# A decoder block on one core: the state-space scan in an order written out by hand, and two memory units in full precision

## The chip, the core and the metric

The kernel runs on one core of a Trainium2 chip. The core has a matrix engine (TensorE, PE in the profile), a vector engine (VectorE, DVE), a scalar engine (ScalarE, ACT) and a general engine (GpSimd, POOL). SyncE (SP) issues most transfers between the main memory and the on-chip memory, SBUF; TensorE writes its results to PSUM. The metric is the device time in microseconds (us). The kernel before takes 1956.74 us as the median of 3 runs (1956.26 to 1957.37).

## The reference

One block of a decoder over 1024 tokens of width 1024, in float32:

```python
def hybrid_mixer(n, w_in, ...):
    z, xBC, dt_raw, q, k, v, r, a1, g_ssd, g_gla = jnp.split(n @ w_in, idx, axis=-1)
    y_ssd = ssd_mixer(z, xBC, dt_raw, ...)
    y_gla = gla_mixer(q, k, v, r, a1, ...)
    merged = sigmoid(g_ssd) * (y_ssd @ w_up_ssd) + sigmoid(g_gla) * (y_gla @ w_up_gla)
    return merged @ w_o

h = h + hybrid_mixer(rmsnorm(h, norm_mix), ...)
h = h + mem_cross_attention(rmsnorm(h, norm_xattn), rmsnorm(mem, norm_mem), ...)
h = h + swiglu(rmsnorm(h, norm_ffn), w_ffn_in, w_ffn_out)
return rmsnorm(h, norm_final)
```

ssd_mixer is a state-space scan: a causal convolution of four taps and a silu over x, B and C; then, chunk by chunk, the masked product of C and B with decay factors exp(cs_t − cs_s) applied to x, plus C times the state carried from the chunks before; a skip term, a gate by silu(z), and an rmsnorm over each of two groups of 512 channels. gla_mixer is a linear attention with a gate per channel, whose logarithm is summed up within chunks. mem_cross_attention attends to 256 fixed memory tokens, whose keys and values come from mem @ w_xkv.

## The kernel before, in words

**Products.** Nearly all matrix products are full-precision products in three passes of a faster number format, fp32r: each operand is split into a high part (a copy by ScalarE, `whi`, line 221) and the rest (a subtraction by DVE, `wlo`), and high×high, high×low and low×high are accumulated. A `Unit` computes 256 output channels for all 1024 tokens by a scheme of seven products instead of eight (B11, B21, T1, B22, T2, T3, T4), each of 12 matmuls of 128x512 into an accumulator `acc`; DVE adds most accumulators into the output (`o<-acc,o`). The weights' sums for the products (`sa`) are made by DVE or POOL.

**Stages.** In the order of the program: the head (memory, x's transposes, keys and values of the memory, and the projection v); the z units, with the preparation of both scans beside them; six xBC units with the convolution; the SSD scan, with units of r, q, k and the first gate unit beside it; the GLA scan, with more gate units; and then the up projections, w_o, cross-attention and feed-forward part.

**The head.** `kv_unit` (line 548) computes 256 of the 2048 key and value columns of the memory. There are eight such units, n = 0 to 7, the values first. `mh` and `ml` are the high and low parts of the memory; a unit splits its weights `raw` in four steps (one `whi` and one `wlo` of 128x512 each) and makes 48 matmuls of 256 columns. Its result goes through `kvs` to the main memory (`vm_d` or `kT_d`). Units 0 and 1 run alone, the next ones beside x's preparation `x_steps`: transposes of x, copies by ScalarE (`xs`), the normed blocks `hs` by DVE, and stores of the copies to `xT_d` by SP. `v_steps` then runs the same seven products for v, with kv units beside it in the banks.

**The scan.** An item is one chunk of 128 tokens of one of the two groups; there are 16. `load` fetches x and z (`xz`), B and C (`bc`) and the running sums of the decay for all partitions (`csb`). `lay` makes C·B and the transposes on TensorE, masks the former into `cbm` and scales x by dt into `xd`. `decay` makes the decay factors `e` (eight ScalarE operations, an exponential), multiplies them by cbm and csb by C. `scan` issues 16 matmuls per kind for the output and two for the state, and updates the state. `gate`, `stat` and `norm` finish the item: skip term and gate (`y`), squares and sums (`sq`, `rd`), a matmul against ones (`stat`), the power by POOL (`rs`), a spreading transpose and the scaling.

**What sets the order.** `run(main, (side, rate))` advances the side generator by `rate` steps for each product of the main units; the tile scheduler then simulates the program and orders the instructions of each engine by priority and readiness, so that the written order is only a starting point. `ahead()` raises the priority of the instructions in it; `pinned` keeps the written order for one instruction. In the scan, 16 items of four steps stand beside nine units of seven products. Tiles with a tag and a number of buffers (`bufs`) are reused in turn: a writer waits for the last reader of the buffer's former content, a transfer among them.

Of the kernel before, what the change touches and what calls it, by code (L numbers as in the profile page):

```python
# [78 lines left out]
def block_kernel(ctx: ExitStack, tc: tile.TileContext, t: dict, out: bass.AP):  # L79
# [467 lines left out]

    def kv_unit(c0):
# [24 lines left out]
        s = stg.tile([P, 2, 256], F32, name="kvs", tag="st")  # L573
# [10 lines left out]
    def x_steps():  # L584
# [4 lines left out]
        for j in range(2):  # L589
# [8 lines left out]
            for k in range(NB):  # L598
# [9 lines left out]
                if k % 4 == 3:  # L608
                    SP.dma_start(xT_d[(k - 3) * P:(k + 1) * P, half(j)].rearrange("(k p) s -> p k s", p=P), xs)
# [26 lines left out]
    def v_steps():  # L636
        for pr in range(2):
# [13 lines left out]
            for n, name in enumerate(CHAIN):  # L651
                parts = []
                with ahead():
# [5 lines left out]
                    elif name == "T3":  # L659
# [123 lines left out]
    def gla_prep():  # L783
# [34 lines left out]
        for h in range(4):  # L818
# [23 lines left out]
    xu = [Unit(w_in, 0, XBC0 + 256 * u) for u in range(6)]  # L842
# [6 lines left out]
    run(singles(zu, B, xu[:1]), (prep, 33 / 28))  # L849
# [4 lines left out]
    cvp = pool("conv", 1, stack=st2)  # L854
    pend = iter(())
    for u in range(6):
        run(group([xu[u]], B, (xu + ru)[u + 1:u + 2]), (pend, 1.0))
        drain(pend)
        pend = conv(u, xu[u])
    drain(pend)  # L860
    st2.close()


    st3 = ExitStack()
    sp_ = pool("ssd", 1, stack=st3)
    state = [sp_.tile([P, GH, 64], F32, name=f"state{g}", tag=f"state{g}") for g in range(2)]
# [5 lines left out]
    class SSD:  # L872
# [8 lines left out]
        def load(s):  # L881
            g, tk = s.g, s.tk
            s.L = sp_.tile([P, 8, CH], F32, name="xz", tag="xz", bufs=3)
            SP.dma_start(s.L[:, 0:4], xbc_d[g * 512:(g + 1) * 512, tk].rearrange("(k p) s -> p k s", p=P))
            s.BC = sp_.tile([P, 2, CH], F32, name="bc", tag="bc", bufs=2)
            for i in range(2):
                r0 = 1024 + i * 256 + g * P
                SP.dma_start(s.BC[:, i], xbc_d[r0:r0 + P, tk])
            s.csb = sp_.tile([P, GH, CH], F32, name="csb", tag="csb", bufs=2)
            SP.dma_start(s.csb.rearrange("p h s -> p (h s)"),  # L890
                         cs_d[s.i0:s.i0 + GH, :].rearrange("h s -> (h s)").partition_broadcast(P))
            SP.dma_start(s.L[:, 4:8], sz_d[g * 512:(g + 1) * 512, tk].rearrange("(k p) s -> p k s", p=P))

        def lay(s):
            p = bank()
# [12 lines left out]
        def decay(s):  # L908
# [8 lines left out]
            mul(DVE, s.e, s.e, s.cbm.unsqueeze(1).to_broadcast([P, GH, CH]))  # L917

        def scan(s):
# [13 lines left out]
            add(DVE, st, p.rearrange("p (h d) -> p h d", d=64), st)  # L933

        def gate(s):
# [5 lines left out]
            sq = sp_.tile([P, 4, CH], F32, name="sq", tag="sq", bufs=1)  # L941
            ACT.activation(sq, s.y, AF.Square)
            s.rd = sp_.tile([P, CH], F32, name="rd", tag="rd", bufs=2)
            add(DVE, sq[:, 0:2], sq[:, 0:2], sq[:, 2:4])
# [14 lines left out]
    def ssd_steps():  # L959
        it = [SSD(c, g) for c in range(NCH) for g in range(2)]  # L960
        it[0].load()
        yield
# [3 lines left out]
        yield  # L966
        for i in range(len(it) + 1):
            z = it[i - 1] if i else None
            a = it[i] if i < len(it) else None
            b = it[i + 1] if i + 1 < len(it) else None  # L970
            if b:
                b.load()
            if a:
                a.scan()
            yield
            if z:
                z.stat()
            if b:
                b.lay()
            yield  # L980
            if a:
                a.gate()
            yield
            if z:
                z.norm()
            if b:
                b.decay()
# [713 lines left out]
```

## Time and profile before

| | |
|---|---|
| median of 3 runs | 1956.74 us |
| profiled execution | 1956.3 us |
| its span on the core | 1954.5 us |
| granted TensorE clock, mean | 0.996 |
| TensorE busy | 1919.9 us (98%) |
| DVE busy | 1317.2 us (67%) |
| ScalarE busy | 848.4 us (43%) |
| POOL busy | 574.1 us (29%) |

The sums in the prediction are made against the profiled execution. A row of a group reads: line, engine, operation, output<-inputs by name, shape, how often, then busy time and mean ns of one, then the engine's idle time just before them and what ended most of it. Nearly every instruction is recorded in a helper, so most rows have line 51 (matmuls), 55 (transposes), 73 (DVE and POOL) or 221 (the high part of a split), and the names tell them apart. The stages in this profile: head with v 0 to 166 us, z units to about 240, xBC units to about 388, SSD scan to about 630, GLA scan to 788, the rest to 1954.

### The profile page before, as it was taken

The page shows a single profiled execution, that of the slowest core. Times are in us where ns is not written, and L with a number is a line of the kernel's source. Part 1 is how long each engine was busy: PE and PEld are TensorE (multiplying, and loading weights), DVE is VectorE, ACT ScalarE, POOL GpSimd, SP SyncE. Part 2 cuts the span into 40 slices and gives each one's busy share as a digit, 9 for nine tenths or more (in the row PEclk, how much of TensorE's full clock was granted, in tenths as well). Part 3 has the DMA queues.
Part 4 walks back from the last instruction along what each step waited for, and adds up shares of the span by engine and source line. Part 5 has one row for each costly group of instructions (what it writes and reads, how often), then busy time and mean ns, then how long its engine had stood idle before and what let it go on. Part 6 is the DMA issues. An engine that isn't in the chain of part 4 may idle for free.

```text
span 1954.5 us, 26271 instructions
## 1 busy us (share of the span) xinstructions
PE 1919.9 (98%) x9772; PEld 1617.3 (83%) x9772; DVE 1317.2 (67%) x1868; ACT 848.4 (43%) x1493; POOL 574.1 (29%) x429
## 2 busy tenths in 40 slices
PE   8899999999999999999999999999999999999998
PEld 7898788778788888888888888888888888888887
DVE  6866779879886655565545237577777777766565
ACT  8434564465552543643224226454333333344243
POOL 1012334355553212112433000006445544320002
PEclk9999999999999999999999999999999999999999
DMA  9333372366553653897684201442233224177463
GB/s 316 139 121 101 119 290 98 133 196 198 169 168 114 209 162 119 328 371 252 242 298 150 78 24 44 140 141 81 87 125 112 82 100 143 42 270 243 159 222 119
DMA packets 238242, 317.97 MB, mean 163 GB/s; under 512 B 16906, under 2 KB 156404, under 8 KB 238116
## 3 DMA queue, kind: packets, MB, share of 16 engines
q1 hardware_dynamic: 238116, 316.31, 47.8%
q8 instruction: 77, 1.26, 0.3%
q14 instruction: 49, 0.40, 0.1%
HBM read 215.27 MB, written 100.99 MB: 162 GB/s over the span
## 4 chain that ended last, share of the span: by engine, by line
PE 83%; DVE 8%; DMA 3%; issue 2%; ACT 2%; POOL 2%; SPq 1%; POOLq 0%; DVEq 0%; ACTq 0%
PE acc L51 72%; PE bank L51 9%; DVE wlo L73 2%; DVE cv L73 1%; PE bank L55 1%; DVE o L73 1%; DMA xt<-in_x_dram 1%; DMA csb<-cs_d 1%; DVE hs L73 1%; DMA raw<-in_w_in_dram 1%; POOL sa L73 0%; ACT e L911 0%; POOL y L73 0%; POOL ssum L73 0%; DVE y L73 0%
## 5 line engine op out<-in xcount | busy, mean ns | idle before, releaser
L51 PE MATMUL acc<-hl,wd 128*128 128x512 f32 x1920 | 438.7, 390 | 0.0
L51 PEld LDWEIGHTS acc<-hl,wd 128*128 128x128 f32 x1920 | 360.4, 188 | 74.1
L73 DVE TENSOR_TENSOR wlo<-raw,whi 128x512 fp32r<-128x512 f32 x272 | 241.6, 894 | 80.7 <-ACT whi L221 78.7
L221 ACT ACTIVATE whi<-raw 128x512 fp32r<-128x512 f32 x272 | 169.5, 628 | 245.1 <-PE acc L51 214.3
L73 DVE TENSOR_TENSOR o<-acc,o 128x512 f32<-128x512 f32 (+1 forms) x256 | 172.8, 676 | 119.8 <-PE acc L51 108.2
L51 PE MATMUL acc<-fs 128*128 128x512 f32 (+1 forms) x792 | 155.7, 356 | 0.1
L51 PEld LDWEIGHTS acc<-fs 128*128 128x128 f32 x792 | 130.8, 189 | 20.7 <-issue 0.5
L73 POOL TENSOR_TENSOR raw<-raw,sa 128x512 f32<-128x512 f32 x44 | 58.7, 1334 | 228.6 <-DVE wlo L73 228.6
L73 DVE TENSOR_TENSOR fs<-fr,fs 128x1024 fp32r<-128x1024 f32 (+1 forms) x84 | 99.0, 1219 | 36.6 <-ACT fs L221 36.5
L221 ACT ACTIVATE fs<-fr 128x1024 fp32r<-128x1024 f32 (+1 forms) x84 | 78.8, 982 | 96.3 <-PE acc L51 32.1
L221 ACT ACTIVATE whi<-sa 128x512 fp32r<-128x512 f32 x96 | 60.0, 626 | 108.3 <-PE acc L51 102.7
L73 POOL TENSOR_TENSOR sa<-raw 128x512 f32<-128x512 f32 x43 | 67.8, 1577 | 105.0 <-DMA raw<-in_w_in_dram 78.0
L73 DVE TENSOR_TENSOR wlo<-sa,whi 128x512 fp32r<-128x512 f32 x96 | 82.2, 857 | 15.2 <-ACT whi L221 15.1
L73 DVE TENSOR_TENSOR wd<-raw,wd 128x1024 fp32r<-128x1024 f32 x40 | 53.1, 1329 | 50.9 <-ACT wd L221 50.8
L73 POOL TENSOR_TENSOR rstd<-rstd,mhalf 128x4 f32<-128x4 f32 (+1 forms) x7 | 8.7, 1246 | 251.2 <-DVE rstd L73 251.2
L221 ACT ACTIVATE wd<-raw 128x1024 fp32r<-128x1024 f32 x40 | 42.3, 1059 | 88.5 <-PE acc L51 82.7
L51 PE MATMUL acc<-B22h,wlo 128*128 128x512 f32 x192 | 76.6, 399 | 3.0 <-DVE wlo L73 3.0
L51 PE MATMUL acc<-T3h,wlo 128*128 128x512 f32 x192 | 76.0, 396 | 1.2 <-DVE wlo L73 1.2
L73 POOL TENSOR_TENSOR raw<-raw 128x512 f32<-128x512 f32 x44 | 75.9, 1725 | 2.8 <-DVE sa L73 2.8
L51 PE MATMUL acc<-T4h,whi 128*128 128x512 f32 x192 | 76.1, 396 | 0.4 <-DVE o L73 0.4
L51 PE MATMUL acc<-B22h,whi 128*128 128x512 f32 x192 | 76.1, 396 | 0.0
L51 PE MATMUL acc<-B11h,whi 128*128 128x512 f32 x192 | 75.8, 395 | 0.0
(389 smaller groups left out, 4735.4 us busy)
## 6 DMA issues: line engine op xcount, KB each, us to landing
raw<-in_w_in_dram SPq DMA_DIRECT2D x26, 1024.0 KB, 5.7
raw<-in_w_ffn_in_dram SPq DMA_DIRECT2D x22, 1024.0 KB, 8.1
act_d<-o SPq DMA_DIRECT2D x77, 256.0 KB, 2.2
fr<-act_d SPq DMA_DIRECT2D x35, 512.0 KB, 5.8
pre<-in_w_ffn_out_dram SPq DMA_DIRECT2D x11, 1024.0 KB
fr<-down_d SPq DMA_DIRECT2D x20, 512.0 KB, 4.7
down_d<-pre SPq DMA_DIRECT2D x33, 256.0 KB, 3.6
raw<-in_w_xkv_dram SPq DMA_DIRECT2D x8, 1024.0 KB, 8.1
```

Of the source, the lines that this page charges most:

```text
L51: return s.e.matmul(o, x, y, **kw)
L55: return s.e.transpose(o, x, i)
L73: return f(*a, **kw)
L221: ACT.activation(hi, src, AF.Copy)
```

## The change

- Head: POOL adds mh and ml into `mf`. kv units 2 and 3 multiply the unsplit weights by mf in full precision: 16 matmuls of 256 columns each, no split. kvs has one buffer instead of three. ScalarE issues the four stores of x's copies instead of SP. v's third difference stands at product T2 instead of T3.
- GLA's preparation makes one scan instruction of 1024 columns for a head instead of two of 512, with one step fewer; the rate beside the z units is 1.0 instead of 33/28.
- The xBC units come in the order 4, 5, 0 to 3 (B and C first), and the first item's data are loaded during the last of them.
- The SSD scan has other steps (some 80 for 70 products), B and C come in one transfer, csb comes a step later, cbm stays in the PSUM bank of C·B, gate and scan are split (gate, square, sum; scan, update). TensorE's instructions keep the written order in this stage. One gate unit moves here from the GLA stage: ten units and five instead of nine and six.

```diff
+    mf = stg.tile([P, NB, MEM], F32, name="mf", tag="mf", bufs=1)
+    for k in range(0, NB, 2):
+        add(POOL, mf[:, k:k + 2], mh[:, k:k + 2], ml[:, k:k + 2])
...
+        whole = n in (2, 3)
         for kk in range(4):
+            if whole:
+                for i in range(2):
+                    o = pa[i][:, :256]
+                    for k in (2 * kk, 2 * kk + 1):
+                        x, y = (raw[:, k], mf[:, k]) if c0 < D else (mf[:, k], raw[:, k])
+                        PE.matmul(o, x[:, i * P:(i + 1) * P], y, start=k == 0, stop=k == 7)
+                yield
+                continue
...
-        s = stg.tile([P, 2, 256], F32, name="kvs", tag="st")
+        s = stg.tile([P, 2, 256], F32, name="kvs", tag="st", bufs=1)
...
-                    SP.dma_start(xT_d[(k - 3) * P:(k + 1) * P, half(j)].rearrange("(k p) s -> p k s", p=P), xs)
+                    ACT.dma_start(xT_d[(k - 3) * P:(k + 1) * P, half(j)].rearrange("(k p) s -> p k s", p=P), xs)
...
-                    elif name == "T3":
+                    elif name == "T2":
                         sub(DVE, A21, A11, A21)
...
-            for j in range(2):
-                pinned(DVE.tensor_tensor_scan(y[:, half(j)], keep[:, half(j)], x[:, half(j)], 0.0, ALU.mult, ALU.add))
-                yield
+            pinned(DVE.tensor_tensor_scan(y, keep, x, 0.0, ALU.mult, ALU.add))
+            yield
...
-    run(singles(zu, B, xu[:1]), (prep, 33 / 28))
+    run(singles(zu, B, xu[:1]), (prep, 1.0))
...
-            s.cbm = sp_.tile([P, CH], F32, name="cbm", tag="cbm", bufs=2)
-            mul(DVE, s.cbm, p[:, :P], triu)
...
-            mul(DVE, s.e, s.e, s.cbm.unsqueeze(1).to_broadcast([P, GH, CH]))
+            cbm = s.p[:, 2 * P:3 * P]
+            mul(DVE, cbm, s.p[:, :P], triu)
+            mul(DVE, s.e, s.e, cbm.unsqueeze(1).to_broadcast([P, GH, CH]))
...
+        for i in range(n + 2):
+            y, z, a, b, c = (it[k] if 0 <= k < n else None for k in range(i - 2, i + 3))
             if a:
                 a.scan()
+            if z:
+                z.sum()
+            if y:
+                y.norm()
+            yield
+            if c:
+                c.load()
+            if b:
+                b.lay()
+            if a:
+                a.gate()
             yield
             if z:
                 z.stat()
             if b:
+                b.decay()
+            if c:
+                c.load_cs()
             if a:
+                a.update()
+            for _ in range(3 if i == 0 else 1):
+                yield
+            if a:
+                a.square()
+                yield
...
-    run(singles(ru + qk + gs[:1], B, gs[1:2]), (ssd, 16 * 4 / 63), prio=PRIO)
+    with tc.manual_schedule(engines={mybir.EngineType.PE}):
+        run(singles(ru + qk + gs[:2], B, gs[2:3]), (ssd, 79 / 70), prio=PRIO)
...
-    run(singles(gs[1:] + gg[:3], B, gg[3:]), (gla, 8 * 5 / 36), prio=PRIO)
+    run(singles(gs[2:] + gg[:3], B, gg[3:]), (gla, 8 * 5 / 30), prio=PRIO)
```

How the instructions move on the engines. First TensorE in the scan, around an item's state matmuls (`xc,bt`), before; `rd` belongs to the norm of the item ahead, `bc` to the next item, `xz` are the transposes of its x:

```order
L51 MATMUL bank<-e,xd 64x128 x2
L51 MATMUL bank<-csb,state_3538 64x128 x2
L51 MATMUL bank<-xc,bt 128x256
L51 MATMUL bank<-ones,rd 128x1
L51 MATMUL bank<-bc 128x128
L55 MATMUL bank<-ident,bc 128x128
L51 MATMUL bank<-xc,bt 128x256
L51 MATMUL acc<-B11h,wlo 128x512
```

After the change, the same place:

```order
L51 MATMUL bank<-e,xd 64x128 x2
L51 MATMUL bank<-csb,state_2552 64x128 x2
L51 MATMUL bank<-xc,bt 128x256 x2
L51 MATMUL bank<-ident,rs 128x128
L51 MATMUL acc<-B11h,whi 128x512
L51 MATMUL acc<-B11l,whi 128x512
L51 MATMUL acc<-B11h,wlo 128x512
```

Before, the scan's matmuls have those of other steps between them, and a product is cut into pieces by the blocks; after, the state's matmuls and the spreading of rs stand together, and then come the 12 matmuls of a whole product, before `bc` and the four transposes of xz; 12 more follow before `ones,rd`, and 12 or 24 before the next scan.

DVE in the scan, before, for one item:

```order
L73 TENSOR_SCALAR rs<-bank 128x1
L73 TENSOR_TENSOR cbm<-bank,triu 128x128
L73 TENSOR_TENSOR e<-e,cbm 128x1024
L73 TENSOR_TENSOR state_3539<-bank,state_3539 128x512
L73 TENSOR_TENSOR o<-acc,o 128x512
L73 TENSOR_TENSOR sq<-sq 128x256
L73 TENSOR_TENSOR rd<-sq 128x128
L73 TENSOR_TENSOR xd<-bank,dtv 128x512
L73 TENSOR_TENSOR o<-acc,o 128x512
```

After:

```order
L73 TENSOR_TENSOR xd<-bank,dtv 128x512
L73 TENSOR_TENSOR wlo<-raw,whi 128x512
L73 TENSOR_TENSOR bank<-bank,triu 128x128
L73 TENSOR_TENSOR o<-acc,o 128x512
L73 TENSOR_TENSOR e<-e,bank 128x1024
L73 TENSOR_SCALAR rs<-bank 128x1
L73 TENSOR_TENSOR state_2551<-bank,state_2551 128x512
L73 TENSOR_TENSOR csb<-csb,bc 128x1024
```

The masked product is now in a bank, and from xd to csb stand eight instructions in one row, of which the next scan needs the last; the sums sq and rd stand outside of it.

In the head, DVE between two groups of splits, before (`hs` are x's normed blocks, `B21l` the low part of a split of them):

```order
L73 TENSOR_TENSOR wlo<-raw,whi 128x512
L73 TENSOR_TENSOR B21l<-hs,B21h 128x512 x2
L73 COPY cols<-bank 128x90
L73 TENSOR_TENSOR hs<-hs 128x512
L73 TENSOR_TENSOR B21l<-hs,B21h 128x512 x2
L73 TENSOR_TENSOR hs<-hs 128x512
L73 SCALAR_TENSOR_TENSOR hs<-xs,cols,rbc 128x512
L73 TENSOR_TENSOR hs<-hs 128x512
L73 SCALAR_TENSOR_TENSOR hs<-xs,cols,rbc 128x512 x2
L73 TENSOR_TENSOR wlo<-raw,whi 128x512
```

After:

```order
L73 TENSOR_TENSOR B21l<-hs,B21h 128x512 x2
L73 TENSOR_TENSOR hs<-hs 128x512
L73 COPY cols<-bank 128x90
L73 SCALAR_TENSOR_TENSOR hs<-xs,cols,rbc 128x512 x3
L73 TENSOR_TENSOR T1l<-hs,T1h 128x512 x4
L73 TENSOR_TENSOR hs<-hs 128x512 x11
L73 TENSOR_TENSOR wlo<-vraw,whi 128x528
L73 TENSOR_TENSOR wlo<-raw,whi 128x512
```

The splits of a kv unit that stood among x's blocks are gone, and the first split of weights comes after the four blocks T1l and eleven differences of hs.

More of the change, by code (lines that the diff above doesn't have):

```diff
@@ L853, in block_kernel @@
     st2 = ExitStack()
[L854 to L861, printed above, removed]
     st3 = ExitStack()
-    sp_ = pool("ssd", 1, stack=st3)
-    state = [sp_.tile([P, GH, 64], F32, name=f"state{g}", tag=f"state{g}") for g in range(2)]
+    sl_ = pool("ssdl", 1, stack=st3)
+    state = [sl_.tile([P, GH, 64], F32, name=f"state{g}", tag=f"state{g}") for g in range(2)]
     for g in range(2):
@@ L959, in ssd_steps @@
     def ssd_steps():
-        it = [SSD(c, g) for c in range(NCH) for g in range(2)]
-        it[0].load()
-        yield
+        n = len(it)
+        it[1].load()
+        it[1].load_cs()
+        for _ in range(1):
+            yield
         it[0].lay()
```

66 lines of the change are left out of this document (38 added, 28 removed).

## The prediction

> **What bounds the kernel now.** I read the page first (shares, chain), then busy time by stage, then each stage's waits. The shares of the span, and the chain that ended last, by engine:
>
> ```profile
> span 1954.5 us, 26271 instructions
> PE 1919.9 (98%) x9772; PEld 1617.3 (83%) x9772; DVE 1317.2 (67%) x1868; ACT 848.4 (43%) x1493; POOL 574.1 (29%) x429
> PE 83%; DVE 8%; DMA 3%; issue 2%; ACT 2%; POOL 2%; SPq 1%; POOLq 0%; DVEq 0%; ACTq 0%
> ```
>
> TensorE is the bound, with 34.6 us idle in all (1954.5 − 1919.9). Busy is not peak, so the stages come next. Windows; columns: stretch and length, then PE, weight load, DVE, ACT, POOL busy us (instructions), granted clock, DMA share, GB/s:
>
> ```profile
> 0.00:40.00 40.00, 31.45 (x237) 28.75 (x237) 20.62 (x37) 33.09 (x65) 3.86 (x12) 1.00 0.91 301
> 40.00:60.00 20.00, 14.13 (x95) 13.56 (x96) 20.00 (x33) 13.81 (x29) 2.84 (x2) 0.84 1.06 376
> 160.00:240.00 80.00, 76.90 (x350) 61.44 (x349) 54.54 (x77) 41.86 (x67) 26.74 (x32) 0.98 0.36 121
> 388.00:600.00 212.00, 208.15 (x1325) 169.73 (x1324) 176.34 (x284) 118.77 (x259) 114.91 (x89) 1.00 0.58 181
> 600.00:788.00 188.00, 188.00 (x942) 159.59 (x941) 110.39 (x220) 81.13 (x195) 48.55 (x40) 1.00 0.47 149
> ```
>
> The change touches 0–60 (head), 160–240 (z units), 388–600 (SSD scan); what follows 788 it leaves alone. The columns alone of the scan do not show what is lost. Same view for the products (tile acc), in the scan and in a stretch of the feed-forward part that never waits; then the chain of waits through one item of the scan:
>
> ```profile
> 388.00:600.00 212.00, 153.34 (x615) 112.99 (x614) 24.47 (x36) 8.64 (x15) 1.00 0.58 181
> 1400.00:1612.00 212.00, 212.00 (x937) 175.70 (x936) 38.35 (x56) 12.75 (x22) 1.00 0.29 97
> 569.64 2.97 PE bank L51 x38
> 572.61 0.11 PE bank L55
> 572.72 0.43 PE bank L51 x2
> 573.15 4.10 PE acc L51 x18
> 577.25 0.44 PE bank L55 x4
> 577.69 0.94 PE acc L51 x4
> 578.62 0.22 PE bank L51 x2
> ```
>
> A product matmul at full rate takes 212/937 = 0.2263 us, so 615 of them need 139.1. An item's own matmuls take 2.97+0.11+0.43+0.44+0.22 = 4.17 us. The tile below has 16 items, the first at 397.3 and the last at 587.7, 12.7 us apart; about 15 fall in the window: 62.6 us. What TensorE loses there is 212 − 139.1 − 62.6 = 10.3 us.
>
> **The scan.** DVE is busy 176 of these 212 us, some 11.8 of each 12.7 us item less the gaps, so it sets which short waits TensorE sees. Groups of DVE (busy, mean ns | idle before), then one tile by min/median/max, then TensorE's waits (sum, count, longest):
>
> ```profile
> L73 DVE TENSOR_TENSOR wlo<-raw,whi 128x512 fp32r<-128x512 f32 x44 | 39.8, 907 | 12.9 <-ACT whi L221 12.9
> L73 DVE TENSOR_TENSOR o<-acc,o 128x512 f32<-128x512 f32 x43 | 29.3, 681 | 12.0 <-PE acc L51 12.0
> L73 DVE TENSOR_TENSOR csb<-csb,bc 128x1024 f32<-128x1024 f32 x16 | 20.0, 1248 | 4.8 <-ACT csb L913 4.7
> L73 DVE TENSOR_TENSOR xd<-bank,dtv 128x512 f32<-128x512 f32 x16 | 10.9, 681 | 0.0
> L73 DVE TENSOR_TENSOR state<-bank,state 128x512 f32<-128x512 f32 x16 | 10.9, 681 | 4.3 <-POOL state L73 4.3
> L73 DVE TENSOR_TENSOR cbm<-bank,triu 128x128 f32<-128x128 f32 x16 | 4.5, 279 | 1.8 <-PE bank L55 1.8
> L73 DVE TENSOR_SCALAR rs<-bank 128x1 f32<-128x1 f32 x16 | 2.4, 148 | 0.2 <-PE bank L51 0.2
> L73 DVE TENSOR_TENSOR e<-e,cbm x16: 1225/2126/2155, 397.3 to 587.7; 128x1024 f32<-128x1024 f32 x16
> PE bank L51 <- POOL rs L73: 2.2, 3, 0.9
> ```
>
> (a) cbm stays in PSUM. The same multiply takes 1.2 us at its quickest and 2.1 at its median; o<-acc,o, with one operand in PSUM, is even. I take 1.25 for e (bounds 1.23 and 2.13): with a mean near 1.94, 0.7 us an item less, 11 us of DVE over 16 items. The page "SBUF — State Buffer" of the Trainium skill, section "Who interferes with whom", says that a DVE instruction with two SBUF inputs contends with a GpSimd instruction that reads SBUF, and one with a single SBUF input does not; the spread of this row agrees, though no run here separates it. By that rule the move to PSUM is worth just this; csb<-csb,bc keeps two SBUF inputs and could inherit the wait.
>
> (b) More room. With ten units (70 products) under 16 items instead of nine, an item has, in the order, 36 or 48 products' matmuls beside it in turn, 42 on average against some 37 before: 42×0.2263+4.17 = 13.7 us for DVE's 11.1. The tenth unit comes from the next stage, where TensorE is busy 188 of 188 us and DVE 110, so nothing is lost or won there.
>
> (c) TensorE's order is fixed as written. Blocks of an item now stand between whole products of 12. In a short item 24 products' matmuls (5.43 us) and the stat matmul lie between the transposes of x and the next scan. In that time DVE does, by its order: xd 0.68, wlo 0.91, the mask multiply 0.28, o 0.68, e 1.25, rs 0.15, the state's update 0.68, csb 1.25: 5.9 us. The scan is then some 0.5 us late in each of the 8 short items (4 us), with about 1 us at the edges: 5 us lost instead of 10.3, **a gain of 5.3**. Bounds: nothing lost, gain 10.3; e at its median of 2.1, 1.4 us late, 8×1.4 = 11.2 lost, 0.9 slower. I take 5 since o, xd and the state's update, each with one operand in PSUM, keep one length beside the same work of POOL, as e now should. Behind a late scan all of TensorE's products stand, and behind those DVE's o; the lateness does not grow, since the long item that follows has 2.7 us (12 matmuls) more than it needs.
>
> (d) The rest: one load fewer an item on SP's queue, item 0's loads moved into the conv stage, the split of gate and scan. The loads land ahead of use now (no DMA among the scan's waits on DVE above), so nothing.
>
> **The head.** TensorE, ScalarE (ACT) and DVE in order of time (start, length, what it waited for), a price of full precision from the GLA stage, and groups of POOL and of stores:
>
> ```profile
> 49.30 0.28 PE L51 MATMUL bank<-whi,mh 128*128 128x256 f32 x1
> 54.85 0.58 PE L51 MATMUL bank<-wlo,mh 128*128 128x256 f32 x1 [5.27 <-DVE wlo L73]
> 55.23 0.42 PE L51 MATMUL bank<-whi,ml 128*128 128x256 f32 x1
> 39.62 2.11 ACT L605 ACTIVATE xs<-bank 128x512 f32<-128x512 f32 x4
> 47.15 0.68 DVE L73 TENSOR_TENSOR wlo<-raw,whi 128x512 fp32r<-128x512 f32 x1
> 54.11 0.68 DVE L73 TENSOR_TENSOR wlo<-raw,whi 128x512 fp32r<-128x512 f32 x1
> 650.90 0.60 PE L51 MATMUL bank<-v,attm 128*128 128x256 f32 x2
> 651.34 0.59 PE L51 MATMUL bank<-sm,qk 128*128 128x256 f32 x2
> L73 POOL TENSOR_TENSOR sa<-sa,raw 128x512 f32<-128x512 f32 x8 | 13.8, 1723 | 0.3
> L582 SPq DMA_DIRECT2D vm_d<-kvs x4: 359/370/3319, 36.5 to 62.8; - x4
> act_d<-o SPq DMA_DIRECT2D x77, 256.0 KB, 2.2
> down_d<-pre SPq DMA_DIRECT2D x33, 256.0 KB, 3.6
> ```
>
> DVE is busy all of 40–60. Between two splits, 47.15 to 54.11, it makes the x blocks, and TensorE waits 5.27 us for the second one. After the hole the matmuls take 0.42–0.58 instead of 0.28, and the window's clock is 0.84. The page "TensorE: Matmul & The Clock Gate", section "What's actually happening", of the Trainium skill says that an idle TensorE drops to half its clock after a few us: the rows agree. By it a hole of 3 to 4 us left behind would cost the slow matmuls too.
>
> Units 2 and 3 in full precision: such a matmul of 256 columns (two records) takes 0.44 us, from the starts 650.90 and 651.34, so a unit takes 16×0.44 = 7.0 us of TensorE against 48×0.113 = 5.4 (half of a 512-wide product). Unit 2's 1.6 us lie in the 8.6 us that TensorE idles before 40; unit 3's in the hole. DVE loses unit 3's four splits, 4×0.68 = 2.7 us, out of the stretch that it fills; unit 2's four went before that. So DVE is some 3 us ahead at the next split that TensorE needs (unit 4's), and **the head ends 3 us sooner**. Upper bound: the hole and its slow clock, 5.27 + 0.75, 6 us; below: nothing, or 1.5 us lost if a hole of the same kind opens in front of unit 4.
>
> Its costs. Four adds for mh+ml on POOL at 1.72 us, 6.9 us, while POOL works 3.9 of the first 40; unit 2 comes behind two units of 5.4 us each and takes the sum two blocks at a time. The kvs buffer is now a single one: ScalarE's copies of unit 1 wait for unit 0's store, issued at 36.5, and those of unit 2 for unit 1's. A store of 256 KB lands 2.2 to 3.6 us after its issue elsewhere, longer perhaps at the DMA share of 1.06 here. By ScalarE's order unit 1's copies now stand behind B11's and beside this run of x's copies (39.62), so the wait is up to 1 us; unit 1's store is then out by 42 to 45, unit 2's copies free its two accumulators at 46 to 49. Until then TensorE has, by its order, 24 matmuls of v, unit 3's 7 us and 12 more of v: from 42 on, some 11 us. Hidden, with 4 us to spare; if that cover goes, v waits for its accumulators and the 3 us go with it. x's four stores leave SP's queue for ScalarE's: 0.4 us each by the issue row, 1.5 us on an engine that works 13.8 of the 20 us; SP's own next loads no longer stand behind them. v's third difference stands earlier in the text, and stood there already in DVE's order: nothing.
>
> **The z units.**
>
> ```profile
> PE acc L51 <- DVE wlo L73: 3.1, 2, 1.9
> L73 DVE TENSOR_TENSOR_SCAN gy<-keep,gx x8: 1199/1216/2244, 213.1 to 248.8; 128x512 f32<-128x512 f32 x8
> ```
>
> One scan of 1024 for two of 512: about 2.4 us either way, but now wlo cannot slip between the halves. The side work also comes later (rate 1.0 for 1.18). Bounds: all of 3.1 gained, or two more waits of 1.2, 2.4 lost; nearest the middle, **0.4 gained**.
>
> **The sum** is against the profiled execution, 1956.3 us (its median of runs is 1956.74, 0.44 above): 1956.3 − 5.3 − 3 − 0.4 = 1947.6; as a median 1948.0.
>
> **The rivals.** A difference of 0.2%, 3.9 us, is about what a measurement of this kernel can tell from none.
> - *More goes.* TensorE's lost 10.3 us vanish as the longer items give DVE 2.6 us of slack each, and the head's hole goes whole: 1956.3 − 10.3 − 6 − 0.4 + 0.4 = 1940. For it: DVE's load falls to 11.1/13.7 = 81%. Against: in the short items the 5.9 us do not fit 5.4.
> - *The holes only move.* e keeps its 2.1 us, or csb takes the contention over: 11.2 lost instead of 10.3; the head saves nothing, since v waits for the kvs stores: about 1957. For it: the median of e is near its maximum, POOL is busy over half of the scan. Against: o<-acc,o's evenness.
> - *The other side: the fixed order stalls TensorE.* Before, products' matmuls stood between the parts of an item's blocks; now a block whose operand is late holds everything behind it. If each of 16 items is 1.6 us late (POOL's rs, up to 0.9 in the row above, with the 0.7 of e), 25.6 are lost for 10.3: 1956.7 + 15.3 − 3.4 = 1969. It decides above (10.3+3.4)/16 = 0.86 us an item, and is slower by 0.2% from 1.1. For it: rs goes through DVE and POOL between two TensorE blocks. Against: between stat and norm now stand 12 or 24 products' matmuls and a scan, 5.7 us or more.
>
> **How the numbers follow.** The forecast 0.50; more goes 0.20; the holes only move 0.13; the stall 0.17. Faster 0.70, same 0.13, slower 0.17. The range takes in the first three: 1937 (1940 less the z units' 3) to 1958 (the moved holes with up to 2 us of the z units' loss).
>
> **What would show it.** In the profile after: e at about 1.25 us, even; TensorE's products in the scan at 42 an item with under 6 us lost by the same sum; the stage one unit longer, the next one shorter; in the head no wait of 5 us on wlo near 50 and a clock above 0.84 in that window; no ScalarE wait over 2 us on the kvs store. I am wrong if TensorE waits for DVE's csb or e by a microsecond in most items, if e stays at 2.1, or if the hole reappears whole at unit 4.

## The result, and the profile after

The changed kernel takes 1962.9 us as the median of 8 runs (1958.75 to 1968.08), the one before 1957.05 us over 8 runs; the ratio is 1.0029, with a 95% interval of 1.0020 to 1.0038. The change makes the kernel 0.3% slower. The forecast was 1948.0 us, in a range of 1937 to 1958.

The profiled execution of the changed kernel is its quickest run, 1958.75 us with a span of 1957.0; the times of the eight runs go with the granted clock, with a mean of 0.996 to 0.998 in the four below 1962 us and of 0.994 or 0.995 in the four above 1964. The page, after: the span, and the busy time of the engines.

```profile
span 1957.0 us, 26169 instructions
PE 1919.1 (98%) x9740; PEld 1617.7 (83%) x9740; DVE 1303.7 (67%) x1856; ACT 845.3 (43%) x1485; POOL 568.7 (29%) x433
```

TensorE idles 37.9 us in all (1957.0 − 1919.1) where it idled 34.6. Windows of the changed kernel, with the columns of the prediction:

```profile
0.00:60.00 60.00, 48.63 (x305) 44.81 (x306) 39.15 (x67) 42.10 (x82) 9.66 (x18) 0.97 0.94 326
160.00:240.00 80.00, 78.35 (x360) 62.65 (x359) 56.24 (x74) 42.31 (x67) 28.32 (x34) 1.00 0.37 124
388.00:620.00 232.00, 223.08 (x1420) 184.37 (x1420) 177.02 (x300) 117.87 (x256) 118.13 (x94) 1.00 0.51 162
800.00:900.00 100.00, 97.57 (x430) 80.23 (x429) 56.34 (x68) 50.62 (x74) 13.06 (x8) 1.00 0.95 347
```

The scan and the stretch behind GLA in the kernel before:

```profile
388.00:620.00 232.00, 228.15 (x1433) 185.87 (x1432) 188.15 (x305) 123.72 (x267) 119.14 (x93) 1.00 0.56 174
800.00:900.00 100.00, 100.00 (x443) 82.86 (x442) 64.99 (x72) 48.67 (x70) 18.38 (x12) 1.00 0.93 343
```

The head and the z units idle less than before (11.4 us for 14.4, the difference of 60.00 and the busy time, and 1.7 for 3.1). The scan idles 8.9 us where it idled 3.9, with 11 us less of DVE's work in it. And after the GLA scan there is a hole that was not there at all. First DVE's multiplies by e and by csb in the scan, after, with its splits of weights (`wlo`), and TensorE's waits there; then TensorE's waits from 640 to 1100:

```profile
L73 DVE TENSOR_TENSOR e<-e,bank x16: 1202/1210/1222, 387.1 to 609.5; 128x1024 f32<-128x1024 f32 x16
L73 DVE TENSOR_TENSOR csb<-csb,bc x15: 1208/1217/2335, 393.3 to 598.4; 128x1024 f32<-128x1024 f32 x15
L73 DVE TENSOR_TENSOR wlo<-raw,whi x41: 677/694/1775, 391.5 to 618.8; 128x512 fp32r<-128x512 f32 x41
PE bank L55 <- issue: 3.9, 3, 1.4
PE bank L55 <- PE bank L55: 1.9, 3, 1.0
PE bank L51 <- issue: 1.3, 1, 1.3
PE bank L51 <- DVE e L73: 1.0, 2, 0.8
```
```profile
PE acc L51 <- ACT wd L221: 2.4, 1, 2.4
```

The multiply by e is even and at 1.21 us, as forecast. But TensorE now waits in front of transposes (line 55), 5.8 us in six places, for something that the profile calls "issue" or a transpose. One such place of the changed kernel in order of time, TensorE and then DVE:

```profile
514.36 0.38 PE L51 MATMUL bank<-ident,rs 128*128 128x128 f32 x2
514.58 0.39 PE L51 MATMUL bank<-bc 128*128 128x128 f32 x2
514.80 0.27 PE L55 MATMUL bank<-ident,bc 128*128 128x128 f32 x1
516.45 0.63 PE L55 MATMUL bank<-ident,xz 128*128 128x128 f32 x4 [1.38 <-issue]
```
```profile
512.48 2.84 DVE L73 TENSOR_TENSOR wlo<-raw,whi 128x512 fp32r<-128x512 f32 x2
515.24 1.11 DVE L73 SCALAR_TENSOR_TENSOR y<-xz,dcol,bank 128x128 f32<-128x128 f32 x4
```

Here the blocks `scan` and `lay` stand in one gap, with no product between them. The four transposes of x want a PSUM bank; the code takes banks in a ring of four, and four takings back it is the scan's output, which DVE's gate (y, line 73) still has to read. DVE is in two splits until 515.3, the gate ends at 516.35, and the transposes start at 516.45. The second of these splits takes 1.75 us, where the quickest takes 0.68. In five of the six places a split of 1.75 to 1.78 us stands right ahead of the gate, and each time POOL works beside it (`raw<-raw`, then the state). Why these splits are so long was not tried by itself.

### The profile page after: what moved, and what is told of

It reads as the page before. It is cut to its first block, busy times and chain, and to the rows that moved or that the text cites. A ratio compares the mean times of both kernels' runs of the same rounds, so it can differ in the third digit from the quotient of the medians.

```text
span 1957.0 us, 26169 instructions
## 1 busy us (share of the span) xinstructions
PE 1919.1 (98%) x9740; PEld 1617.7 (83%) x9740; DVE 1303.7 (67%) x1856; ACT 845.3 (43%) x1485; POOL 568.7 (29%) x433
## 4 chain that ended last, share of the span: by engine, by line
PE 83%; DVE 6%; DMA 5%; ACT 3%; issue 2%; POOL 1%; SPq 1%; ACTq 0%; POOLq 0%; DVEq 0%
PE acc L51 71%; PE bank L51 10%; DVE wlo L73 2%; PE bank L55 1%; DVE cv L73 1%; DMA xt<-in_x_dram 1%; DVE o L73 1%; DMA h_d<-ga 1%; DMA xT_d<-xs 1%; ACT e L915 1%; DMA hl<-ys_d 1%; POOL ssum L73 1%; DMA pre<-in_w_ffn_out_dram 0%; DMA csb<-cs_d 0%; ACT whi L221 0%
## 5 line engine op out<-in xcount | busy, mean ns | idle before, releaser
L221 ACT ACTIVATE whi<-raw 128x512 fp32r<-128x512 f32 x264 | 164.9, 628 | 249.2 <-PE acc L51 208.0
L51 PE MATMUL acc<-T1h,whi 128*128 128x512 f32 x192 | 76.1, 396 | 0.0
L51 PE MATMUL acc<-T3h,whi 128*128 128x512 f32 x192 | 75.9, 395 | 0.0
```

Source lines behind the costliest of these rows:

```text
L51: return s.e.matmul(o, x, y, **kw)
L221: ACT.activation(hi, src, AF.Copy)
```

## The experiments

The times are medians; each kernel is compared with the kernel before on the same chip, which had 1955.2 to 1957.1 us there.

**The three parts alone.** Each is the kernel before with one part of the diff shown above: the head (mf, the two whole kv units, kvs with one buffer, x's stores by ScalarE, v's difference); the scan (order of the xBC units, loads, steps, fixed order, ten and five units); and the z units (one scan instruction of 1024, and the rate):

```diff
-            for j in range(2):
-                pinned(DVE.tensor_tensor_scan(y[:, half(j)], keep[:, half(j)], x[:, half(j)], 0.0, ALU.mult, ALU.add))
-                yield
+            pinned(DVE.tensor_tensor_scan(y, keep, x, 0.0, ALU.mult, ALU.add))
+            yield
...
-    run(singles(zu, B, xu[:1]), (prep, 33 / 28))
+    run(singles(zu, B, xu[:1]), (prep, 1.0))
```

> The kernel before with the head's part of the change alone. Theory A (read from the two profiles: the head ends 1.0 us sooner, the z units 2.5 us more, and the scan with the seam behind GLA gives 6 back): about 1 us faster than before, the same spread as before. Rival B (the changed head sometimes drops the clock, and this is why eight runs of the changed kernel spread over 9 us where those of before spread over 4): 3 to 5 us slower at the median with a spread of some 9 us.

> The kernel before with the scan's part alone (order of the xBC units, loads, steps, fixed order of TensorE, ten units and five; the rate beside the z units stays 33/28). Theory A: 6 us slower than before or more, since TensorE waits for the transposes of x behind a bank that DVE frees late (about 1 us in some eight items) and for 2.6 us at the seam behind GLA. Rival B: no more than 2 us slower, with the spread of before.

> The kernel before with the one scan instruction of 1024 columns and the rate of 1.0 beside the z units. Both theories: TensorE waits of 5 us around 220 to 226 become half, 2.5 us faster. If only the rate mattered in company with other parts: within 1 us of before.

Measured: the head 1955.56 us, ratio 0.9994 (0.9985 to 1.0002); the scan 1963.83, 1.0037 (1.0025 to 1.0049); the z units 1955.31, 0.9993 (0.9985 to 1.0002). The scan's part, to which the seam behind GLA belongs, carries the whole loss, 7.5 us, and the other two about 1 us of gain each, which their intervals do not separate from none. The sum is within a microsecond of the whole change. The head's twelve runs spread over 8.7 us, which its rival B had, but not the 3 to 5 us at the median that went with it.

**The fixed order taken away**, all else as changed.

```diff
-    with tc.manual_schedule(engines={mybir.EngineType.PE}):
-        run(singles(ru + qk + gs[:2], B, gs[2:3]), (ssd, 79 / 70), prio=PRIO)
+    run(singles(ru + qk + gs[:2], B, gs[2:3]), (ssd, 79 / 70), prio=PRIO)
```

> The changed kernel with the scheduler's own order of TensorE in the scan instead of the written one. Theory A: the waits of 0.9 to 1.5 us in front of the transposes of x go, 4 to 7 us faster than the changed kernel and so about 1957. Rival C (the loss lies in the new steps and in the move of a unit, not in the fixed order): within 2 us of the changed kernel.

Measured: 1944.31 us (1940.27 to 1947.2), ratio 0.9936 (0.9923 to 0.9949): 18 us below the changed kernel by the two ratios, more than expected. Its window of the scan has no idle at all:

```profile
388.00:620.00 232.00, 232.00 (x1470) 192.85 (x1470) 182.66 (x312) 121.34 (x261) 116.45 (x100) 1.00 0.53 167
```

DVE does more there in the same time than in the changed kernel (182.7 us for 177.0), which fits that it no longer waits for a TensorE that waits. In its trace 8 to 17 product matmuls stand between an item's C·B and its transposes of x in 12 of 15 items, where the written order has none.

**Is it the fixed order itself, or its pace?** A rate of 79/70 owes a second step within one gap now and then, and makes every other item short. With eleven units and a rate of 1.0 every item has scan, 12, transposes, 12, stat, 24.

```diff
-        run(singles(ru + qk + gs[:2], B, gs[2:3]), (ssd, 79 / 70), prio=PRIO)
+        run(singles(ru + qk + gs[:3], B, gs[3:4]), (ssd, 1.0), prio=PRIO)
...
-    run(singles(gs[2:] + gg[:3], B, gg[3:]), (gla, 8 * 5 / 30), prio=PRIO)
+    run(singles(gs[3:] + gg[:3], B, gg[3:]), (gla, 8 * 5 / 24), prio=PRIO)
```

> The changed kernel, TensorE's order fixed, but with eleven units and a rate of 1.0 in the scan's stage (four units in the next), so that no two steps of the scan share a gap between products and every item is a long one: scan, 12, transposes, 12, stat, 24. Theory A (the fixed order loses where an item is short or two steps stand in one gap): TensorE's waits in front of the transposes of x go, and the time comes to within 4 us of the kernel with the scheduler's own order, 1944 to 1948. Rival (a fixed order loses by itself, at any pace): it stays above 1956.

Measured: 1953.76 us, ratio 0.9995. The time lies between the two expectations; the windows tell why (scan, GLA stage, the stage behind it), and TensorE's waits from 640 to 1100 in this kernel:

```profile
388.00:620.00 232.00, 231.90 (x1443) 193.28 (x1443) 175.19 (x301) 118.74 (x254) 117.64 (x95) 1.00 0.52 165
620.00:800.00 180.00, 176.87 (x885) 150.22 (x883) 109.43 (x219) 87.93 (x197) 39.24 (x34) 0.99 0.61 202
800.00:900.00 100.00, 96.44 (x415) 78.73 (x416) 49.15 (x60) 43.11 (x67) 23.76 (x16) 0.97 0.86 308
```
```profile
PE acc L51 <- ACT wd L221: 3.0, 2, 2.0
PE bank L55 <- ACT o L1110: 2.6, 1, 2.6
PE bank L55 <- DVE S L73: 1.1, 1, 1.1
```

The fixed order at an even pace idles 0.1 us in the scan, and the scheduler's order at the changed kernel's pace none. So it takes both to make TensorE wait, the fixed order and the changed kernel's pace. This run, and the next pair, also give every item 48 product matmuls where the changed kernel gives 42 on average: whether the evenness or the length helps is not separated. What is given back lies at the seam behind GLA, 6.7 us (3.1 + 3.6), where four units are too few to stand beside the GLA scan.

The same even pace with ten units needs five steps fewer at the start; once with the fixed order, once with the scheduler's.

```diff
-        for _ in range(6):
+        for _ in range(3):
             yield
...
-            for _ in range(3 if i == 0 else 1):
+            for _ in range(1):
                 yield
...
-        run(singles(ru + qk + gs[:2], B, gs[2:3]), (ssd, 79 / 70), prio=PRIO)
+        run(singles(ru + qk + gs[:2], B, gs[2:3]), (ssd, 1.0), prio=PRIO)
```

> The changed kernel with the fixed order and its ten and five units, but one step for each product: a rate of 1.0, and five steps fewer at the start, so that every item has scan, 12, transposes, 12, stat, 24 and the last steps fall into the next stage. Theory A: TensorE's waits in the scan go as they did with eleven units, and the seam behind GLA is no worse than in the changed kernel (2.6 us), so 1944 to 1950. Rival: the waits come back somewhere else, above 1955.

> The same even steps with the scheduler's own order. Theory A: the scheduler had no stalls left in the scan to take away, so within 3 us of 1944, and no better than the fixed order at the same pace by more than 3 us.

Measured: 1964.18 us (fixed, ratio 1.0030) and 1955.53 us (scheduler's, 0.9995). Theory A failed on both times and held on the scan with the fixed order; for that run the rival held, waits that come back somewhere else. TensorE's waits from 370 to 1100, fixed order:

```profile
PE bank L51 <- DVE e L73: 6.5, 1, 6.5
PE acc L51 <- ACT wd L221: 6.5, 1, 6.5
PE bank L55 <- ACT o L1110: 1.9, 1, 1.9
PE acc L51 <- DVE wd L73: 1.7, 2, 1.4
```

There is no wait between the first item and the end of the scan. But the shortened start makes the first item wait 6.5 us for its e, and the seam costs 6.5 and more, in both orders (with the scheduler's TensorE waits 6.4 us for `wd` there too): the scan's last steps had been pushed into the next stage, and GLA's last products of v and k (`v,kt`) start at 801 us instead of 791 with the fixed order.

**The seam: the unit moved back**, the fixed order kept, and the same with the scheduler's order.

```diff
-        run(singles(ru + qk + gs[:2], B, gs[2:3]), (ssd, 79 / 70), prio=PRIO)
+        run(singles(ru + qk + gs[:1], B, gs[1:2]), (ssd, 79 / 63), prio=PRIO)
...
-    run(singles(gs[2:] + gg[:3], B, gg[3:]), (gla, 8 * 5 / 30), prio=PRIO)
+    run(singles(gs[1:] + gg[:3], B, gg[3:]), (gla, 8 * 5 / 36), prio=PRIO)
```

> The changed kernel with TensorE's order fixed, but nine units in the scan's stage and six in the next, the rates raised to fit. Theory A: the seam's 2.6 us go, as GLA has a unit more beside it; but items become shorter and more of them have two steps in one gap, so that the scan's waits grow by more than that: 1963 to 1972. If the seam is the larger part: below 1960.

> The scheduler's own order in the scan with the new steps, but nine units in this stage and six in the next as before, the rate raised to fit. By term (b) of the prediction (an item has 42 matmuls beside it instead of 37, so that DVE has room) TensorE loses some 5 us again, about 1949; if the new steps and the PSUM product alone give the gain, within 2 us of 1944.

Measured: 1952.87 us with the fixed order (ratio 0.9985, 0.9973 to 0.9997) and 1941.88 us with the scheduler's (0.9920, 0.9907 to 0.9934). Theory A failed in the first, whose second expectation, below 1960, held; in the second the loss by term (b) did not come. By the ratios the kernel with ten and five units is 8.6 us slower under the fixed order (1.0029 against 0.9985) and 3.1 under the scheduler's (0.9936 against 0.9920), where the intervals overlap. The scan and the stage behind GLA with the fixed order, then the scan with the scheduler's:

```profile
388.00:620.00 232.00, 225.94 (x1434) 188.34 (x1435) 179.15 (x306) 116.00 (x250) 114.49 (x95) 0.99 0.52 165
800.00:900.00 100.00, 100.00 (x443) 82.81 (x442) 60.86 (x71) 45.64 (x68) 20.07 (x12) 1.00 0.92 341
```
```profile
388.00:620.00 232.00, 229.86 (x1456) 190.74 (x1456) 184.75 (x318) 119.13 (x254) 117.16 (x100) 1.00 0.56 174
```

The seam's idle is gone in both; with the scheduler's order, too, TensorE is busy for all of 800 to 900. With the fixed order the scan still idles 6.1 us, 4.9 of it in one wait in front of transposes; with the scheduler's 2.1. So shorter items did not wait more under the fixed order, and of three items after the first with scan and transposes in one gap only one waited: how short the gaps are does not settle the waits alone. The scheduler's version is the fastest kernel of the study, 0.8% below the one before. That the moved unit costs anything there is not shown: in the profiles TensorE needs 1126.9 us from the first product of the z units to the last on `wd` with nine units and 1125.6 with ten, and what the profile with nine units gains is the head, which ends 2.8 us sooner.

**The changed kernel, a second time**, for a profile of a usual run.

> The changed kernel once more, for a second profile. Its first one was of its quickest run, 1958.75 us against a median of 1962.9. Theory A (the scan's waits and the seam are in every run, the rest of the spread is the clock in the head): the waits in the scan between 400 and 640 us are again 17 to 19 us in sum, and what is longer than in the first profile lies before 160 us. Rival: the longer run has longer waits in the scan or at the seam.

Measured: two runs of 1965.3 and 1969.1 us; the profile has a span of 1963.6, 6.6 us more than the first. The scan's window and the stretch from 900 to 1100, second profile, and TensorE's waits from 640 to 1100 in it:

```profile
388.00:620.00 232.00, 222.41 (x1418) 183.95 (x1415) 173.80 (x298) 117.00 (x254) 115.80 (x93) 1.00 0.50 160
900.00:1100.00 200.00, 196.92 (x863) 162.26 (x862) 96.25 (x107) 58.91 (x84) 72.91 (x51) 0.98 0.66 223
```
```profile
PE acc L51 <- ACT wd L221: 4.7, 2, 2.8
```

Neither theory had the place. The scan is much the same (9.6 us idle for 8.9) and the head no slower: the z units start at 163.8 us for 164.3. The difference is in the up projections and w_o, which the change does not touch: a second wait for `wd`, near 1042 us, and a granted clock of 0.98 for 1.00 in the window around it. The idle time there is 2.5 us more; the clock's two hundredths of 200 us are some 4 by estimate. There ScalarE waits for POOL's sums, and POOL works on the feed-forward weights (`pre`), whose first load the changed kernel issues at 831 us and the one before at 810. The first load of that preparation, before, after, and in the fastest kernel:

```profile
L1255 SPq DMA_DIRECT2D pre<-in_w_ffn_out_dram x11: 383/384/508, 809.7 to 1014.1; - x11
```
```profile
L1296 SPq DMA_DIRECT2D pre<-in_w_ffn_out_dram x11: 383/383/461, 830.9 to 1020.7; - x11
```
```profile
L1296 SPq DMA_DIRECT2D pre<-in_w_ffn_out_dram x11: 383/384/1523, 790.4 to 997.6; - x11
```

That the late start of this preparation is why POOL is late at 1042 fits the order of events, but it is not enough: in the run on the bank, next, the preparation starts at 834 us, and TensorE is busy for 199.97 of the 200 us from 900 to 1100.

**The bank.** The spreading of rs written ahead of the scan's matmuls, so that the transposes of x take over its bank and not the scan's output.

```diff
-            if a:
-                a.scan()
-            if z:
-                z.sum()
             if y:
                 y.norm()
+            if a:
+                a.scan()
+            if z:
+                z.sum()
             yield
```

> The changed kernel with the spreading of rs written ahead of the scan's matmuls instead of behind them; then the transposes of x take over the PSUM bank of this spreading and no longer that of the scan's output. Theory A in its form on the bank (TensorE waits for DVE's gate because of that bank): the waits of 0.9 to 1.9 us in front of the transposes go, some 8 us faster than the changed kernel, about 1955. Rival: the wait is for something else, or goes to rs in front of the scan: within 3 us of the changed kernel.

Measured: 1961.59 us, ratio 1.0034: the rival. TensorE's waits in its scan:

```profile
PE bank L51 <- POOL rs L73: 2.8, 3, 1.8
PE bank L51 <- DVE y L73: 2.7, 2, 1.4
```

The waits in front of the transposes (line 55) are down to 0.2 us, and as much waits in front of stat and rs instead. The bank is the form that the wait takes; behind it stands an item's work on DVE and POOL, which is not finished by the time that the fixed order asks for it.

**The old steps with a fixed order.** The kernel before, with only `manual_schedule` around its scan.

> The kernel before with nothing changed but TensorE's order in the scan fixed as written. If the fixed order is what costs, the kernel before loses too, and more than the changed one, since its items have 36 matmuls on average: over 10 us slower than before. If only the new steps and a fixed order together cost: within 4 us of before.

Measured: 1969.69 us, ratio 1.0059. The time is over 10 us slower as expected, but by luck: the loss is one wait, ahead of the first item, whose B and C come from the last convolutions.

```profile
PE bank L51 <- DMA bc<-xbc_d: 14.3, 1, 14.3
```
```profile
388.00:620.00 232.00, 231.05 (x1428) 192.28 (x1429) 175.91 (x298) 124.18 (x269) 111.01 (x89) 0.99 0.53 169
```

Inside the scan the old steps in fixed order, at a rate of 64/63 and so nearly even, with 48 product matmuls an item and not the expected 36, idle 1 us where the scheduler's order idled 3.9.

**cbm back in SBUF**, with the scheduler's order.

> The scheduler's own order in the scan, with the masked product cbm in SBUF again as before the change. By term (a) of the prediction the multiply by e is back at 1.9 us in the mean and TensorE loses up to 5 us, so 1946 to 1949; if the looser pace alone gives DVE the room, the multiply is slow again but the time stays within 2 us of 1944.

Measured: 1946.76 us, ratio 0.9959 (0.9947 to 0.9971), 2.5 us above the same kernel with cbm in PSUM by the medians; the two intervals touch. The time is as expected; the multiply by e is uneven again, though its mean is 1.65 us and not 1.9. First with cbm in SBUF, then in PSUM, both with the scheduler's order:

```profile
L73 DVE TENSOR_TENSOR e<-e,cbm x16: 1211/1556/2311, 385.1 to 592.6; 128x1024 f32<-128x1024 f32 x16
```
```profile
L73 DVE TENSOR_TENSOR e<-e,bank x16: 1203/1221/1222, 386.8 to 588.0; 128x1024 f32<-128x1024 f32 x16
```

**The head.** In the fastest kernel with the old head, and the head alone a second time.

> The fastest version so far (the scheduler's own order, nine and six units, 1941.9 us), but with the head as it was before the change. By the profiles the changed head saves 3 us, so 1944 to 1946; by the runs of the head alone it saves 0.8, so 1942 to 1943.5.

> The kernel before with the head's part alone, once more, for a second profile. If the head's runs spread because TensorE's wait at 55 to 57 us sometimes lasts long enough to halve the clock, this profile differs from the first in the granted clock between 40 and 80 us and by as many us of span.

Measured: 1948.02 us with the old head (0.9953, 0.9940 to 0.9965), where the fastest kernel has 0.9920; the spans of the profiles are 1944.3 and 1941.7. The head alone again: 1955.39 us (0.9997, 0.9987 to 1.0007), span 1951.6; the first profile had 1952.2, the kernel before 1954.5. So by spans the head saves 2.3, 2.9 and 2.6 us, by medians 0.8 to 1 alone and 6.5 in company, by the ratios. The second profile does not differ from the first in the way that was expected: both have a granted clock of 1.00 from 60 to 65 us, and the z units start at 161.9 us in both. Over all twelve profiles with this head the clock does tell: where it is 1.00 from 60 to 65 us (six profiles) the z units start at 161.4 to 162.3 us, and where it is 0.59 to 0.85 (six) at 163.1 to 164.8; the kernel before has 165.3. The length of TensorE's wait for kvs does not tell which it will be: 3.0 us stand before a clock of 1.00 in one, 1.8 before 0.69 in the changed kernel. Whether this is why the medians and the spans disagree stays open.

**The values' stores by ScalarE**, with the scheduler's order: one line, `SP.dma_start(vm_d...` to `ACT.dma_start(vm_d...`.

> The scheduler's own order in the scan, and the four stores of the memory's values issued by ScalarE instead of SP. If TensorE's 2 to 3 us wait for the single kvs buffer at 55 to 57 us comes from SP's late stores, it goes, and the time is 2 us below the 1944 of the scheduler's own order; if it comes from ScalarE's order (unit 2's copies stand behind x's blocks, which wait for the store of x), the wait stays and the time with it.

Measured: 1955.31 us, ratio 1.0001: 11 us worse than without this line by the medians, which neither expectation had. The z units start 12.1 us later (176.8 us for 164.7). ScalarE's longest wait from 15 to 60 us, and the store's issue in order of time:

```profile
ACT hs L604 <- DMA vraw<-in_w_in_dram: 15.2, 1, 15.2
```
```profile
35.74 0.40 ACTq L595 DMA_DIRECT2D vm_d<-kvs  x1
```

ScalarE stands for 15 us in front of its own store, until a load on another queue has landed; x's preparation is queued behind it. In the trace that load of `vraw`, issued at 29.62 us, and the store signal the same semaphore, and the wait is for this one. So the store most likely waited for a semaphore in use, as the program was built, and not for its data; that was not tried. The question on the kvs wait is not answered by this run.

## Why the prediction was wrong

**Right.** (a) The multiply by e takes 1.21 us, evenly, as the 1.25 of the prediction had it, and csb did not take the contention over (median 1.22, one at 2.3). The page "SBUF — State Buffer" of the Trainium skill, section "Who interferes with whom", says that a DVE instruction with at most one SBUF input, outside the 2-port perf modes, does not contend with GpSimd: with cbm in SBUF the same multiply, under the scheduler's order too, reached 2.31, in PSUM 1.22, so the runs agree with it. The z units gave 1.0 us by medians for a forecast of 0.4, both within the noise. The head's 3 us are what the spans show (2.3 to 2.9) where the clock stays up behind it, but only 1 us of it is in the median of the head alone, and the changed kernel's own profiles have the z units start only 1.0 and 1.5 us sooner than before.

**The step that failed most: (c), the 0.5 us for each short item.** It counted what DVE must do between the transposes of x and the next scan, and took the transposes as starting on time. They did not: they wait for the gate of the item ahead, by way of a PSUM bank, 5.8 us in all; the scan itself waits for e just twice, 1.0 us. And two steps sometimes fall into one gap, as in the rows at 514 us (no products between the spreading of rs and `bc`): a short item has its 36 matmuls, as the prediction counted them, but not always 24 of them behind the transposes. The list of DVE's work has one split at the mean of 0.91, where those ahead of the gate took up to 1.78. What TensorE loses in 388 to 600, counted alike for the three kernels: an item has 47 matmul records of its own (38, 1, 2, 4 and 2 in the prediction's rows), so the records that are no products give the items. Before, 710 records are 15.1 items, and 212 − 139.2 − 63.0 = 9.8 us. After, 625 product matmuls at 0.2263 are 141.4 and 685 records are 14.6 items or 60.8 us: 9.8 again, for a forecast of 5. So none of the 5.3 us came. Before, 3.9 of the 9.8 us are idle, after 7.9; the rest is time that counts as busy in which TensorE does less. The rows for this sum, all matmuls and then the products, after and with the scheduler's order:

```profile
388.00:600.00 212.00, 204.06 (x1310) 168.90 (x1309) 160.43 (x270) 113.65 (x248) 108.81 (x87) 1.00 0.52 168
388.00:600.00 212.00, 152.14 (x625) 114.54 (x624) 25.35 (x37) 9.24 (x16) 1.00 0.52 168
```
```profile
388.00:600.00 212.00, 212.00 (x1379) 176.21 (x1379) 168.76 (x290) 115.32 (x251) 110.00 (x93) 1.00 0.54 171
388.00:600.00 212.00, 156.28 (x642) 117.85 (x642) 25.96 (x38) 9.27 (x16) 1.00 0.54 171
```

With the scheduler's order, 642 matmuls are 145.3 and 737 records are 15.7 items or 65.4 us: 1.3 lost. That is the rival "more goes" in the scan, which the fixed order kept away. The rival of the other side had the right mechanism, something late that holds everything behind it, but put 1.6 us into every item and had the operand e or rs late; here it is mostly the output bank, in six items, and at an even pace of 48 matmuls an item it does not occur. A smaller slip: DVE's 11.8 us an item divides all of its 176 us by 15 items, though 212 us are 16.7 times 12.7; it is 10.6.

**The second: (b), "nothing is lost or won there" for the moved unit.** TensorE was busy 188 of 188 us in GLA, and the prediction read this as room. It was cover: the GLA scan is a chain of its own that needs products beside it until its end. With one unit fewer, and the scan's end later (the last `ys_d` store at 639 us for 631), GLA's end lies behind the products', and the next stage's weights wait: 2.4 us in the first profile, 1.9 in the second; with two units fewer the idle time from 620 to 900 is 6.7. It takes both: with the scheduler's order and the same ten and five units the last store is at 622 us, and TensorE is busy for all of 800 to 900. Moving the unit back, with the rates, gave 8.6 us with the fixed order; in the profiles TensorE idles 2.9 us less in the scan and 2.4 less from 800 to 900 than in the first profile of the changed kernel.

The whole by one measure: from the first product of the z units to the last on `wd` TensorE needs 1136.0 us before, 1139.5 and 1146.6 in the two profiles of the changed kernel, and 1125.6 with the scheduler's order. The forecast for this stretch was 5.7 us less than before.

**The head's cover** was priced as hidden with 4 us to spare. TensorE did wait for kvs, 1.8 us at 57, but not for the store of kvs:

```profile
56.44 2.19 ACT L221 ACTIVATE B22h<-hs 128x512 fp32r<-128x512 f32 x4 [5.34 <-DMA xT_d<-xs]
58.53 0.82 ACT L591 ACTIVATE kvs<-acc,mss 128x256 f32<-128x256 f32 x2
```

Unit 2's copies stand behind B22's blocks in ScalarE's order, and these wait for the store of x out of the buffer that they take over. The prediction counted the stores' issue on ScalarE, 0.4 us each, and not who waits for their landing. Its upper bound for the head is too small: before, 25 matmuls from 55.23 to 60.56 us start 0.213 us apart instead of 0.119, so the slow clock behind the hole cost some 2.4 us and not 0.75.

## What to carry to other kernels

A written order on an engine that runs in order holds everything behind a block that is not ready: list the gaps of every item, not their mean, and check for each block whether its inputs and its output bank are free by then. An engine that is 100% busy in a stage may be the cover of a chain beside it; before work is moved out of the stage, see when that chain ends and what the next stage waits for. A change that is slower as a whole can hold a faster one: without the fixed order this one is 0.6% faster than the kernel before.

## What the runs showed of the chip that was not expected

A store issued by ScalarE held ScalarE for 15.2 us, until a load on SP's queue that signals the same semaphore had landed, while x's four stores, moved to the same engine in the changed kernel, held it for nothing of that size. After the wait of 14.3 us in the old steps with a fixed order, the granted clock was 0.50 from 388 to 392 us, and the product matmuls took 0.63 to 0.78 us instead of 0.39, until 394 us:

```profile
373.70 0.39 PE L51 MATMUL acc<-T2h,wlo 128*128 128x512 f32 x1
388.41 0.77 PE L51 MATMUL bank<-bc 128*128 128x128 f32 x2 [14.32 <-DMA bc<-xbc_d]
390.47 0.63 PE L51 MATMUL acc<-T1l,whi 128*128 128x512 f32 x1
```
